# Two halves of side work in one step: transposes of a block, levels of a linear head, and a softmax head behind the last one

## The chip, the cores and the metric

The kernel runs on one core of a Trainium2 chip, in fp32 (the large products in a split form of two fp32r parts). The metric is the device time of one execution in microseconds (us), the median over executions; less is better. Names of engines: PE is TensorE, ACT is ScalarE, DVE is VectorE, POOL is GpSimd, SP is SyncE.

## The reference

Two blocks follow each other on 256 tokens of width 2048. The first has two layers, each a projection, three mixers (chunked band attention with 8 heads, gated linear attention with 4, memory attention with 4), an output projection and a layer norm. The second has a linear mixer (hgrn2, 8 heads), a softmax mixer (fox, 8 heads), a gated merge, and a feed-forward part (FFN).

```python
x = first_block(x, mem, w_in, ...)            # 2 layers
h = rms_norm(x, norm_mix_pre)
a_q, a_f, a_i, a_g, b_q, b_k, b_v, b_f, g_a, g_b = split(h @ w_in_2)
y_a = hgrn2_mixer(a_q, a_f, a_i, a_g, lb, norm_w) @ w_up_a
y_b = fox_mixer(b_q, b_k, b_v, b_f + b_fox_f) @ w_up_b
merged = sigmoid(g_a) * y_a + sigmoid(g_b) * y_b
x = x + rms_norm(merged @ w_o, norm_mix_post)
gate, up = split(rms_norm(x, norm_ffn_pre) @ w_ffn_in)
x = x + rms_norm((silu(gate) * up) @ w_ffn_down, norm_ffn_post)
# hgrn2_mixer: f = lb + (1-lb)*sigmoid(z), k = 1-f, S_t = diag(f_t) S_{t-1} + k_t^T i_t, o_t = S_t^T q_t
```

## The kernel before

All large products are one list of jobs, and `run` walks it in units. A unit is some 2.7 us of PE work: 12 rows of matmuls (lines L330 to L332) or 16 rows (L339, L340). Weights come by SP's queue; ACT rounds them to fp32r (L272) and DVE takes the rest (L273), some units ahead of their use.

Everything else is side work, written as Python generators. Each `yield d` gives up the turn and asks for the next one after `d` on a clock that `run` adds up from matmul columns (about ns of PE). After every unit `pump` lets at most two generators that are due take one step, so a step's matmuls stand between two units in PE's queue, and its other instructions go to the ends of the queues of ACT, DVE and POOL at that point. No scheduler moves them later: each engine works its queue in the order in which it was written. Side work writes to a pool of four PSUM banks that rotate (`B.bank()`): the fifth bank asked for is the first again, and its writer waits until that one has been read.

The side work around which the change turns:

- `hgrn_head` (8 heads of the second block, each in two halves t of 128 tokens). For each t: `decay_levels` puts ten POOL operations (L674 to L684) and two on ACT (absolute value L685, exponential L686) to make a tile E of eight levels; `H1` later 14 POOL products (L766, L767, "the set" below) and one more (L770 or L772); `H2` later eight PE products with E, four to a bank, each bank then masked on DVE (L782); then a DVE sum (L785), a product with the values, and `normed`: a square on ACT (L692), a power on POOL (L447), a scaling on DVE (L694), and, `R3` later, a transpose on PE (L377).
- `post_f` takes the forget gate's projection from PSUM: copy on ACT (L472), two DVE operations (L473, L484), two sigmoids on ACT (L1238, L1239), three POOL operations (L1243, L1244, L1245, "the trio" below). It is called twice per group of four heads, directly behind its product.
- `banded` and `memory_head`, softmax heads in three steps: scores and softmax, a transpose of the weights, the product with the values. Two generators of two heads each form a group.
- `merged` and `hidden`: a block of 512 columns of 256 rows is transposed in two halves of four transposes (`to_features`).

Of the kernel before, what the change touches and what calls it, by code (L numbers as in the profile page):

```python
# [52 lines left out]
R2 = 3500  # L53
# [327 lines left out]
def network(ctx, tc, a):  # L381
# [12 lines left out]
    def lv(i):  # L394
        return s(i).rearrange("p (l t) -> p l t", l=8)
# [31 lines left out]
    def main_split(src, k0, k1, cols=slice(0, S), scale=None):  # L427
        B.split_to(B.act[:, k0:k1, 0, cols], B.act[:, k0:k1, 1, cols], src, scale)
# [174 lines left out]
    def banded(q, k, v, bias, out):  # L603

        yield from B.acquire("att")
        st = B.bank()
        parts = (slice(0, 128), slice(128, 384))
        for t, cs in enumerate(parts):
            qs, ks = slice(t * P, t * P + P), slice(0, t * P + P)
            T.matmul(st[:, cs], q[:, qs], k[:, ks], start=True, stop=True)  # L610
        pt = B.ttile([P, 512], "P", N_ATT)
        nm, sm, rc = (B.stile([P, 2], x) for x in ("nm", "sm", "rc"))
        for i, cs in enumerate(parts):
            V.tensor_tensor_reduce(pt[:, cs], st[:, cs], bias(i, pt[:, cs]), -1.0, 3e38, ALU.add, ALU.min, nm[:, i:i + 1])
        for i, cs in enumerate(parts):
            A.activation(pt[:, cs], pt[:, cs], AF.Exp, bias=nm[:, i:i + 1], scale=-1.0, accum_out=sm[:, i:i + 1])
        V.reciprocal(rc, sm)
        for i, cs in enumerate(parts):
            V.tensor_scalar(pt[:, cs], pt[:, cs], rc[:, i:i + 1], None, ALU.mult)
        yield A1  # L620
        tb = B.bank()
        for j in range(3):
            T.transpose(tb[:, j * P:(j + 1) * P], pt[:, j * P:(j + 1) * P], ident)
        A.copy(pt[:, :384], tb[:, :384])
        yield A2
        ob = B.bank()
        T.matmul(ob[:, 0:128], v(0), pt[:, 0:128], start=True, stop=True)
        T.matmul(ob[:, 128:256], v(0), pt[:, 128:256], start=True, stop=False)
        T.matmul(ob[:, 128:256], v(1), pt[:, 256:384], start=False, stop=True)
        out(ob[:, :S])  # L630
        B.tokens["att"] += 1
        yield

    def memory_head(q, mk, mv, out):
        yield from B.acquire("att")
        st = B.bank()
        for t in range(2):
            T.matmul(st[:, t * S:(t + 1) * S], q[:, t * P:t * P + P], mk, start=True, stop=True)
        pt = B.ttile([P, 512], "P", N_ATT)
        nm, sm, rc = (B.stile([P, 2], x) for x in ("nm", "sm", "rc"))  # L640
        V.tensor_reduce(nm, st.rearrange("p (t m) -> p t m", t=2), AX.X, ALU.max, negate=True)
        for t in range(2):
            cs = slice(t * S, (t + 1) * S)
            A.activation(pt[:, cs], st[:, cs], AF.Exp, bias=nm[:, t:t + 1], accum_out=sm[:, t:t + 1])
        V.reciprocal(rc, sm)
        for t in range(2):
            cs = slice(t * S, (t + 1) * S)
            V.tensor_scalar(pt[:, cs], pt[:, cs], rc[:, t:t + 1], None, ALU.mult)
        yield A1
        tb = B.bank()  # L650
        for m in range(2):
            for t in range(2):
                T.transpose(tb[:, m * S + t * P:m * S + t * P + P], pt[:, t * S + m * P:t * S + m * P + P], ident)
        A.copy(pt, tb)
        yield A2
        ob = B.bank()
        for m in range(2):
            T.matmul(ob[:, :S], mv(m), pt[:, m * S:(m + 1) * S], start=m == 0, stop=m == 1)
        out(ob[:, :S])
        B.tokens["att"] += 1  # L660
        yield

# [2 lines left out]
    def decay_levels(E, b, t, scale):  # L667

        bt = b[:, t * P:(t + 1) * P]
        for l in range(6):  # L670
            st = 1 << l
            view = lambda x: x.rearrange("p (n u) -> p n u", u=2 * st)
            ref = view(bt)[:, :, st - 1:st].to_broadcast([P, P // (2 * st), 2 * st])
            G.tensor_tensor(view(E[:, l, :]), view(bt), ref, ALU.subtract)  # L674
        end = lambda c: b[:, c * 64 + 63:c * 64 + 64]
        lo, hi = slice(0, 64), slice(64, 128)
        G.tensor_scalar(E[:, 6, lo], bt[:, lo], end(2 * t), None, ALU.subtract)
        G.tensor_copy(E[:, 6, hi], bt[:, hi])
        if t == 0:
            G.tensor_scalar(E[:, 7, lo], bt[:, lo], end(0), end(1), ALU.subtract, ALU.subtract)  # L680
            G.tensor_scalar(E[:, 7, hi], bt[:, hi], end(1), None, ALU.subtract)
        else:
            G.tensor_copy(E[:, 7, lo], bt[:, lo])
            G.tensor_scalar(E[:, 7, hi], bt[:, hi], end(2), None, ALU.add)  # L684
        A.activation(E, E, AF.Abs)  # L685
        A.activation(E, E, AF.Exp, scale=-scale)  # L686
# [65 lines left out]
    def hgrn_head(q, k, b, v, mask, gain, out):  # L752

        yield from B.acquire("lin")
        for t in range(2):
            while len(B.free) < 3:
                yield 2000
            (ei,) = B.alloc(1)
            E = lv(ei)
            ts = slice(t * P, (t + 1) * P)  # L760
            decay_levels(E, b, t, 1.0)
            yield H1
            for l in range(7):
                view = lambda x: x.rearrange("p (n h u) -> p n h u", h=2, u=1 << l)
                e = view(E[:, l, :])
                G.tensor_tensor(e[:, :, 0, :], e[:, :, 0, :], view(k[:, ts])[:, :, 0, :], ALU.mult)  # L766
                G.tensor_tensor(e[:, :, 1, :], e[:, :, 1, :], view(q[:, ts])[:, :, 1, :], ALU.mult)  # L767
            if t == 0:
                kx = B.ttile([P, P], "kx", N_LIN)
                G.tensor_tensor(kx, E[:, 7, :], k[:, ts], ALU.mult)  # L770
            else:
                G.tensor_tensor(E[:, 7, :], E[:, 7, :], q[:, ts], ALU.mult)  # L772
            yield H2
            (mi,) = B.alloc(1)
            ms = lv(mi)
            for half in range(2):
                bank = B.bank().rearrange("p (l t) -> p l t", l=4)
                ls = slice(4 * half, 4 * half + 4)
                for l in range(4 * half, 4 * half + 4):
                    kk, qq = (E[:, l, :], E[:, l, :]) if l < 7 else (k[:, ts], q[:, ts])  # L780
                    T.matmul(bank[:, l % 4, :], kk, qq, start=True, stop=True)
                V.tensor_tensor(ms[:, ls, :], bank, mask[:, ls, :], ALU.mult)  # L782
                yield R2
            sc = B.ttile([P, 2, P], "sc", N_LIN)
            V.tensor_reduce(sc[:, 0, :], ms.rearrange("p l t -> p t l"), AX.X, ALU.add)  # L785
            if t == 1:
                cross = B.ttile([P, 2, P], "cross", N_LIN)[:, 0, :]
                xb = B.bank()
                T.matmul(xb[:, :P], kx, E[:, 7, :], start=True, stop=True)
                A.copy(cross, xb[:, :P])  # L790
            B.release([ei, mi])
            yield R1
            ob = B.bank().rearrange("p (e v) -> p e v", v=P)
            T.matmul(ob[:, 0, :], sc[:, 0, :], v(t), start=True, stop=t == 0)
            if t == 1:
                T.matmul(ob[:, 0, :], cross, v(0), start=False, stop=True)
            yield from normed(ob, sc, 1, gain, out(t))
        B.tokens["lin"] += 1
# [586 lines left out]
    def to_features(gi, n):  # L1385

        bank = B.bank()
        for j in range(2):
            for t in range(2):
                T.transpose(bank[:, (2 * j + t) * P:(2 * j + t + 1) * P],  # L1390
                            vt(gi)[:, t, (2 * n + j) * P:(2 * n + j + 1) * P], ident)
        return bank.rearrange("p (k t) -> p k t", t=S)
# [3 lines left out]
    def merged(c):  # L1396
        yield FH
        for n in range(2):
            main_split(to_features(st[f"gb{c}"], n), 4 * c + 2 * n, 4 * c + 2 * n + 2, scale=0.5)
            yield 1500  # L1400
        B.release([st[f"gb{c}"]])

    def merged_get(kt):
# [140 lines left out]
    def hidden(c, gi):  # L1544

        yield FH
        if len(f["h"]) <= 2 * c:
            f["h"] += B.alloc(2, F32R)
        for n in range(2):
            slot_split(f["h"][2 * c + n:2 * c + n + 1], to_features(gi, n))  # L1550
            yield 1500
        B.release([gi])

    def hidden_get(kt):
# [92 lines left out]
```

## Time and profile before

| | |
|---|---|
| time, median of 3 runs | 2407.39 us (2406.78 to 2407.83) |
| the profiled execution's own time | 2407.96 us |
| its span, first to last instruction | 2406.2 us |
| PE busy | 2390.2 us (99%) |
| PE weight loads busy | 2015.7 us (84%) |
| DVE busy | 1476.3 us (61%) |
| ACT busy | 1099.0 us (46%) |
| POOL busy | 400.8 us (17%) |
| DMA | 464.64 MB, mean 193 GB/s |
| granted PE clock | 0.999 of full |

Busy time is the sum of an engine's instructions. PE's queue holds the jobs and the side work together, so each of its gaps lengthens the execution; gaps of the other engines need not. "PE row" and a number below count the main matmuls from the start of the program (10768 in all), which places a side step in both orders.

### The profile page before, as it was taken

How to read it: one execution, taken by the hardware profiler on the slowest of the kernel's cores; microseconds unless marked ns; L12 is line 12 of the kernel's file. 1: busy time of each engine (PE TensorE's matmuls, PEld its weight loads, DVE VectorE, ACT ScalarE, POOL GpSimd, SP SyncE). 2: the span in 40 equal slices, each digit the busy share in tenths (PEclk: the TensorE clock that was granted, in tenths of full speed). 3: DMA queues.
4: the chain of work that ended last, by engine and by line, in shares of the span. 5: the costliest groups of instructions: out<-in, count | busy, mean ns of one | idle time of the engine just before them, and what ended most of it. 6: DMA issues, size and time to landing. Idle time of an engine off the chain costs nothing. (4 is left out here: it accounts for less than half of the span.)

```text
span 2406.2 us, 31460 instructions
## 1 busy us (share of the span) xinstructions
PE 2390.2 (99%) x12105; PEld 2015.7 (84%) x12105; DVE 1476.3 (61%) x1671; ACT 1099.0 (46%) x1472; POOL 400.8 (17%) x601
## 2 busy tenths in 40 slices
PE   9999999999999999999999999999999999999998
PEld 8888888888888888888888888888888888888886
DVE  6587567666855667766765656657545544554455
ACT  6444445345454553655544544445434423443433
POOL 0330010004400110364764340001000000000000
PEclk9999999999999999999999999999999999999999
DMA  9646567674656674854654666675755655555653
GB/s 327 184 149 184 173 187 262 209 239 133 188 160 186 206 252 156 275 164 125 185 161 146 201 185 194 202 242 186 242 176 180 194 185 193 201 183 177 209 192 131
DMA packets 313911, 464.64 MB, mean 193 GB/s; under 512 B 21961, under 2 KB 161569, under 8 KB 313761
## 3 DMA queue, kind: packets, MB, share of 16 engines
q1 hardware_dynamic: 312528, 459.48, 60.7%
q8 instruction: 95, 1.56, 0.3%
q0 software_dynamic: 640, 2.10, 0.2%
q10 hardware_dynamic: 592, 1.06, 0.1%
q14 instruction: 56, 0.45, 0.1%
HBM read 454.18 MB, written 8.40 MB: 192 GB/s over the span
## 5 line engine op out<-in xcount | busy, mean ns | idle before, releaser
L273 DVE TENSOR_TENSOR slot<-slot,slot 128x1024 fp32r<-128x1024 f32 x810 | 1006.9, 1287 | 190.5 <-ACT slot L272 186.7
L272 ACT CAST slot<-slot 128x1024 fp32r<-128x1024 f32 x810 | 807.8, 1046 | 266.2 <-DVE slot L273 123.6
L339 PE MATMUL main_j<-act,slot 128*128 128x512 f32 x1824 | 651.0, 400 | 0.0
L330 PE MATMUL main_j<-slot,act 128*128 128x512 f32 x1608 | 636.2, 396 | 0.0
L331 PE MATMUL main_j<-slot,act 128*128 128x512 f32 x1608 | 626.4, 390 | 2.8 <-DVE slot L273 2.8
L332 PE MATMUL main_j<-slot,act 128*128 128x512 f32 x1608 | 626.8, 390 | 0.0
L340 PE MATMUL main_j<-act,slot 128*128 128x256 f32 x1824 | 509.9, 280 | 0.0
L339 PEld LDWEIGHTS main_j<-act,slot 128*128 128x128 f32 x1824 | 342.4, 188 | 80.2 <-issue 1.1
L331 PEld LDWEIGHTS main_j<-slot,act 128*128 128x128 f32 x1608 | 302.4, 188 | 63.6 <-DVE slot L273 3.8
L332 PEld LDWEIGHTS main_j<-slot,act 128*128 128x128 f32 x1608 | 301.8, 188 | 63.9
L330 PEld LDWEIGHTS main_j<-slot,act 128*128 128x128 f32 x1608 | 302.2, 188 | 61.3 <-ACT slot L272 0.5
L340 PEld LDWEIGHTS main_j<-act,slot 128*128 128x128 f32 x1824 | 344.1, 189 | 0.8
L330 PE MATMUL main_j<-slot,slot 128*128 128x512 f32 x600 | 236.1, 394 | 0.0
L332 PE MATMUL main_j<-slot,slot 128*128 128x512 f32 x600 | 233.8, 390 | 0.0
L331 PE MATMUL main_j<-slot,slot 128*128 128x512 f32 x600 | 233.6, 389 | 0.0
L447 POOL TENSOR_TENSOR rsl<-rsl,nhalf 128x1 f32<-128x1 f32 x8 | 6.2, 775 | 991.7 <-DVE rsl L446 991.7
L332 PEld LDWEIGHTS main_j<-slot,slot 128*128 128x128 f32 x600 | 112.6, 188 | 23.8
L330 PEld LDWEIGHTS main_j<-slot,slot 128*128 128x128 f32 x600 | 112.7, 188 | 23.0
L331 PEld LDWEIGHTS main_j<-slot,slot 128*128 128x128 f32 x600 | 112.8, 188 | 22.5
L674 POOL TENSOR_TENSOR slot<-slot 128x128 f32<-128x128 f32 x144 | 79.2, 581 | 191.9 <-PE main_j L339 92.8
L354 ACT CAST slot<-bank 128x512 fp32r<-128x512 f32 (+1 forms) x30 | 15.9, 529 | 177.7 <-PE bank L377 170.7
L813 POOL TENSOR_TENSOR slot<-slot,tz 128x512 f32<-128x512 f32 x20 | 25.8, 1290 | 397.8 <-DVE tz L812 397.8
(193 smaller groups left out, 1738.4 us busy)
## 6 DMA issues: line engine op xcount, KB each, us to landing
slot<-in_w_in_dram SPq DMA_DIRECT2D x384, 512.0 KB, 4.0
slot<-in_w_ffn_in_dram SPq DMA_DIRECT2D x176, 512.0 KB, 4.6
slot<-in_w_ffn_down_dram SPq DMA_DIRECT2D x88, 512.0 KB, 4.6
slot<-in_w_out_dram SPq DMA_DIRECT2D x64, 512.0 KB, 4.7
slot<-in_w_o_dram SPq DMA_DIRECT2D x32, 512.0 KB, 4.5
slot<-in_w_mem_kv_dram SPq DMA_DIRECT2D x31, 512.0 KB, 5.9
slot<-in_w_up_b_dram SPq DMA_DIRECT2D x16, 512.0 KB, 4.6
slot<-in_w_up_a_dram SPq DMA_DIRECT2D x16, 512.0 KB, 4.4
```

Of the source, the lines that this page charges most:

```text
L272: nc.scalar.copy(h, src)
L273: nc.vector.tensor_tensor(l, src, h.bitcast(F32), ALU.subtract)
L330: nc.tensor.matmul(o, xh[:, rows], h[:, k, :], start=st, stop=False)
L331: nc.tensor.matmul(o, xh[:, rows], l[:, k, :], start=False, stop=False)
L332: nc.tensor.matmul(o, xl[:, rows], h[:, k, :], start=False, stop=en)
L339: nc.tensor.matmul(job.ps[:, f, :], h[:, k, fs], xs, start=st, stop=False)
L340: nc.tensor.matmul(job.ps[:, f, :S], l[:, k, fs], xh, start=False, stop=en)
L354: nc.scalar.copy(h, src)
L447: G.tensor_tensor(out, out, nhalf[:, :n], ALU.pow)
L674: G.tensor_tensor(view(E[:, l, :]), view(bt), ref, ALU.subtract)
L813: G.tensor_tensor(y, y, tz, ALU.mult)
```

## The change

Five `yield`s go or move, and nothing else. The two halves of a transposed block (`merged`, `hidden`) are written in one step, with a bank each. The two halves of the levels in `hgrn_head` are written in one step, and the delay `R2` (3500) follows once instead of twice. The last `yield` of `banded` and `memory_head` goes, so a generator's second head writes its scores in the same step as the first head's last product.

```diff
@@ banded, memory_head
         out(ob[:, :S])
         B.tokens["att"] += 1
-        yield
@@ hgrn_head
                 V.tensor_tensor(ms[:, ls, :], bank, mask[:, ls, :], ALU.mult)
-                yield R2
+            yield R2
             sc = B.ttile([P, 2, P], "sc", N_LIN)
@@ merged
             main_split(to_features(st[f"gb{c}"], n), 4 * c + 2 * n, 4 * c + 2 * n + 2, scale=0.5)
-            yield 1500
@@ hidden
             slot_split(f["h"][2 * c + n:2 * c + n + 1], to_features(gi, n))
-            yield 1500
```

Line numbers of `hgrn_head` and what follows are two lower in the changed kernel (L766 is L764 there, L1243 is L1241). Number and kind of the instructions on each engine stay as they were; their order changes from PE row 968 on, and the number of stretches of side work in PE's queue falls from 211 to 176.

Three places in the second block carry the steps below. The first is PE's queue at a levels step. Before, the four levels of E tile 1634 stand at PE row 5344 and the other four at row 5392, with three main units between them:

```order
L340 MATMUL main_j76_10083<-act_72,slot_1655_9887 128x256
L373 MATMUL bank_1690_10101<-slot_1634_9769 128x128 x4
L339 MATMUL main_j76_10083<-act_72,slot_1665_9935 128x512
...
L340 MATMUL main_j76_10083<-act_72,slot_1676_10010 128x256
L373 MATMUL bank_1707_10208<-slot_1634_9769 128x128 x3
L373 MATMUL bank_1707_10208<-slot_1494_8875,slot_1466_8676 128x128
L339 MATMUL main_j77_10220<-act_72,slot_1679_10036 128x512
```

After the change all eight of the same head's tile, now numbered 1680, stand at row 5392, in two banks:

```order
L340 MATMUL main_j76_10136<-act_72,slot_1689_10064 128x256
L373 MATMUL bank_1718_10267<-slot_1680_10010 128x128 x4
L373 MATMUL bank_1719_10273<-slot_1680_10010 128x128 x3
L373 MATMUL bank_1719_10273<-slot_1494_8875,slot_1466_8676 128x128
L339 MATMUL main_j77_10285<-act_72,slot_1692_10091 128x512
```

The second place is POOL's queue at the two calls of `post_f` of the second group (PE rows 5264 and 5328). Before, a decay group of ten operations stands ahead of the first trio, and between the two trios there are one power and one set:

```order
L674 TENSOR_TENSOR slot_1634_9769<-slot_1467_8677 128x128 x6
L677 TENSOR_SCALAR slot_1634_9769<-slot_1467_8677 128x64
...
L1243 TENSOR_TENSOR slot_1657_9908<-slot_1657_9908,om_1464_8672 128x512
L1244 TENSOR_TENSOR slot_1657_9908<-slot_1657_9908,lb_1463_8671 128x512
L1245 TENSOR_TENSOR slot_1658_9909<-slot_1658_9909,om_1464_8672 128x512
L447 TENSOR_TENSOR rs_1670_9961<-rs_1670_9961,nhalf_117 128x1
L766 TENSOR_TENSOR slot_1634_9769<-slot_1634_9769,slot_1466_8676 128x64
```

After it, a power and a decay group (tile 1680) stand between the trios, and the set of 1680 stands behind the second trio, followed by the next head's decay group (1709) and then a power:

```order
L1243 TENSOR_TENSOR slot_1671_9963<-slot_1671_9963,om_1464_8672 128x512
L447 TENSOR_TENSOR rs_1675_9977<-rs_1675_9977,nhalf_117 128x1
L672 TENSOR_TENSOR slot_1680_10010<-slot_1467_8677 128x128 x6
...
L1243 TENSOR_TENSOR slot_1671_9963<-slot_1671_9963,om_1464_8672 128x512
L764 TENSOR_TENSOR slot_1680_10010<-slot_1680_10010,slot_1466_8676 128x64
...
L770 TENSOR_TENSOR slot_1680_10010<-slot_1680_10010,slot_1494_8875 128x128
L672 TENSOR_TENSOR slot_1709_10218<-slot_1467_8677 128x128 x6
...
L447 TENSOR_TENSOR rs_1712_10235<-rs_1712_10235,nhalf_117 128x1
```

The third place is ACT's queue between the two calls of `post_f`. Before, no absolute value or exponential of a decay group stands between the first call's sigmoids and the second call's copy (L472); there are weight casts, a softmax head's exponentials and a square:

```order
L1239 ACTIVATE slot_1658_9909<-slot_1659_9910 128x512
L616 ACT_TABLE_LOAD
L616 ACTIVATE P_1661_9922,sm_1663_9924<-P_1661_9922,nm_1662_9923 128x128
L616 ACTIVATE P_1661_9922,sm_1663_9924<-P_1661_9922,nm_1662_9923 128x256
L272 CAST slot_1665_9935<-slot_1637_9786 128x1024
L692 ACTIVATE sc_1638_9805,ss_1669_9960<-bank_1668_9958 128x128
```

After it, the absolute value and the exponential of tile 1680 (L683, L684) stand there, ahead of three weight casts, two copies out of banks and the copy for the second call; the square of the next half (L690) stands behind the pair of tile 1709 in the same way further down the queue:

```order
L272 CAST slot_1677_9987<-slot_1650_9831 128x1024
L683 ACTIVATE slot_1680_10010<-slot_1680_10010 128x1024
L684 ACT_TABLE_LOAD
L684 ACTIVATE slot_1680_10010<-slot_1680_10010 128x1024
L272 CAST slot_1681_10023<-slot_1656_9860 128x1024
L624 COPY P_1659_9887<-bank_1687_10058 128x384
L272 CAST slot_1688_10063<-slot_1665_9919 128x1024
L354 CAST slot_1587_9522<-bank_1691_10085 128x256
L272 CAST slot_1692_10091<-slot_1669_9944 128x1024
L472 COPY slot_1672_9964<-main_j75_9993 128x512
...
L684 ACTIVATE slot_1709_10218<-slot_1709_10218 128x1024
L690 ACTIVATE sc_1696_10124,ss_1711_10234<-bank_1710_10231 128x128
```

## Rows read from the trace of the kernel before

**Rows 1.** Windows: us, then busy us and count of each engine, clock, DMA

```profile
100.00:960.00 860.00, 860.00 (x4748) 736.68 (x4747) 575.48 (x679) 402.43 (x590) 132.34 (x139) 1.00 0.62 191
1700.00:2390.00 690.00, 690.00 (x3087) 571.27 (x3086) 352.51 (x340) 272.57 (x302) 0.55 (x1) 1.00 0.59 189
```

**Rows 2.** Waits of PE by releaser: total us, times, longest

```profile
PE bank L377 <- DVE sc L694: 1.7, 1, 1.7
...
PE bank L373 <- POOL slot L767: 0.7, 1, 0.7
```

**Rows 3.** Timeline of PE in the FFN: start, us, instruction

```profile
1716.72 0.39 PE L332 MATMUL main_j<-slot,act 128*128 128x512 f32 x1
1716.96 0.60 PE L377 MATMUL bank<-ident,slot 128*128 128x128 f32 x4
...
1717.62 0.40 PE L331 MATMUL main_j<-slot,act 128*128 128x512 f32 x1
```

**Rows 4.** Timeline of PE in the second block

```profile
1125.24 0.38 PE L373 MATMUL bank<-slot,sc 128*128 128x128 f32 x2
...
1128.28 0.83 PE L373 MATMUL bank<-slot 128*128 128x128 f32 x6
1128.95 0.39 PE L373 MATMUL bank<-slot,slot 128*128 128x128 f32 x2
```

**Rows 5.** Timeline of ACT in the second block

```profile
1127.30 0.58 ACT L472 COPY slot<-main_j 128x512 f32<-128x512 f32 x1
...
1131.50 1.28 ACT L616 ACT_TABLE_LOAD   x1
1132.79 0.40 ACT L616 ACTIVATE P<-P,nm 128x128 f32<-128x128 f32 x1
...
1134.63 0.26 ACT L692 ACTIVATE sc<-bank 128x128 f32<-128x128 f32 x1
...
1136.76 0.47 ACT L624 COPY P<-bank 128x384 f32<-128x384 f32 x1
1137.13 1.05 ACT L272 CAST slot<-slot 128x1024 fp32r<-128x1024 f32 x1
1138.09 0.58 ACT L472 COPY slot<-main_j 128x512 f32<-128x512 f32 x1
```

**Rows 6.** Timeline of DVE in the second block

```profile
1127.16 0.68 DVE L782 TENSOR_TENSOR slot<-bank,slot 128x512 f32<-128x512 f32 x1
1127.76 1.21 DVE L273 TENSOR_TENSOR slot<-slot,slot 128x1024 fp32r<-128x1024 f32 x1
...
1136.72 0.29 DVE L694 TENSOR_TENSOR sc<-bank,rs 128x128 f32<-128x128 f32 x1 [0.68 <-POOL rs L447]
```

**Rows 7.** Timeline of POOL in the second block

```profile
1031.44 4.26 POOL L674 TENSOR_TENSOR slot<-slot 128x128 f32<-128x128 f32 x6 [19.03 <-DVE slot L1260]
...
1040.90 0.36 POOL L766 TENSOR_TENSOR slot<-slot,slot 128x64 f32<-128x64 f32 x1 [3.61 <-ACT slot L686]
...
1046.92 0.45 POOL L770 TENSOR_TENSOR kx<-slot,slot 128x128 f32<-128x128 f32 x1
...
1096.49 2.22 POOL L674 TENSOR_TENSOR slot<-slot 128x128 f32<-128x128 f32 x6
...
1102.24 0.36 POOL L766 TENSOR_TENSOR slot<-slot,slot 128x64 f32<-128x64 f32 x1 [2.33 <-ACT slot L686]
...
1111.19 0.46 POOL L772 TENSOR_TENSOR slot<-slot,slot 128x128 f32<-128x128 f32 x1
...
1133.37 1.04 POOL L1245 TENSOR_TENSOR slot<-slot,om 128x512 f32<-128x512 f32 x1
1136.12 0.57 POOL L447 TENSOR_TENSOR rs<-rs,nhalf 128x1 f32<-128x1 f32 x1 [1.71 <-DVE rs L446]
...
1144.19 0.46 POOL L772 TENSOR_TENSOR slot<-slot,slot 128x128 f32<-128x128 f32 x1
...
1147.60 2.02 POOL L1245 TENSOR_TENSOR slot<-slot,om 128x512 f32<-128x512 f32 x1
```

More of the change, by code (lines that the diff above doesn't have):

```diff
@@ L660, in memory_head @@
         B.tokens["att"] += 1
-        yield
     def decay_levels(E, b, t, scale):
```

## Prediction, made before the changed kernel ran

> **What bounds the kernel now.** I read the windows first. From 100 to 960 us and from 1700 to 2390 us PE is busy for all of the 860 and 690 us, at the full one of its two clock levels, 2.4 GHz [rows 1]. Nothing can be won in those stretches except by shortening PE's own list; every wait that an edit adds to PE's queue there, or in the second block between them, is added to the time. Then I read who PE waits for. In the second block's mixers it waits twice: 1.7 us for the scaling L694 and 0.7 us for a product of a set, L767 [rows 2]. These 2.4 us are all that the change could remove there. PE runs a fixed list, so the question is whether side work that stands earlier in that list is still ready in time.
>
> **What costs next to nothing.** The change adds and removes no instruction. It takes 35 stretches of side work out of PE's queue (211 to 176, counted in the orders). What does a stretch cost beside its matmuls? In the FFN 0.90 us pass from one main matmul (1716.72) over four transposes and the next one to the second behind them (1717.62), and a main step is 0.24, up to 1716.96 [rows 3]: 0.42 us are left for four transposes and all else. A fp32 side matmul of 128 columns takes 0.22 us (three, recorded as six, in 0.67, from 1128.28 to 1128.95 [rows 4]); a transpose is recorded once where such a matmul is recorded twice, so 0.11, and four fill the 0.42. I take 0.02 for a stretch, 0.7 us for 35, and allow from nothing to 0.05, 1.8 us.
>
> `merged` and `hidden` (15 steps) now put eight transposes in a row, which use two of the four side banks. Their input has to be ready at the same point as before, since the first half already needed both row halves. What hides the second half's copies on ACT and DVE is the lead of the weights: in the new order a cast L272 stands 48 to 64 PE rows ahead of the first matmul that reads it, some 10 us. If that cover were gone, each step would cost one more bank copy, about 0.47 us by the nearest row (L624, [rows 5]), 7 us in all; PE's 690 us without a gap speak against it [rows 1].
>
> The softmax heads' scores come one unit earlier. They read only q and k, long there, and in the first block PE has no gap now. The jobs that drain those heads come several units after the last step in both orders. I take zero, with up to 3 us where the scores of two heads and a levels step follow each other at PE rows 5916 to 5940 and share four banks.
>
> **Where it costs: the levels of the linear heads.** Eight levels in one step want the whole set of POOL products at the point where so far only half was wanted, and two banks at once. Since `R2` is paid once, each half of a head also ends one or two units earlier, and the next head's decay group moves up in POOL's and ACT's queues. The place where this meets something is around the two trios of the second group. I count from T, the moment when PE ends the job at PE row 5264.
>
> PE's own way. Sixteen rows take 2.82 us: from the matmul at 1125.24 (0.22) to the next side step at 1128.28 is 3.04 [rows 4]. With 0.22 for a side matmul, from row 5264 to 5328 stand 64 rows (11.3) and the side work of rows 5264, 5296 and 5312 (0.75 + 2.05 + 0.65; a transpose 0.11): PE comes to its step at row 5328 at T + 14.8.
>
> Wait A, row 5328. The step's transpose takes the bank that the first four levels of row 5296 filled, four banks ago; DVE must have masked them (L782). In DVE's order a weight operation L273 stands ahead of that, and waits for a cast that in ACT's order stands behind the absolute value and exponential of tile 1680. These wait for 1680's decay group, which on POOL stands behind the first trio and a power. From the copy L472 to the end of the trio the trace shows 7.1 us (1127.30 [rows 5] to 1134.41 [rows 7]); the power 0.57; from a decay group's first operation to the first product that reads the exponential 5.75 (1096.49 to 1102.24 [rows 7]), without a table load, which is another 1.28 [rows 5]: 7.0. Then a cast 1.05 [rows 5], L273 1.21 and L782 0.68 [rows 6]. 7.1 + 0.57 + 7.0 + 1.05 + 1.21 + 0.68 = 17.6. Wait A: 17.6 - 14.8 = 2.8 us. Bounds: 0.5 (no table load, and no L273 inside the trio's way, 1.0), and 7.2, if the trio takes the 11.5 us of the second call before (1138.09 [rows 5] to 1149.62 [rows 7]).
>
> Wait B, row 5392. After the exponential (T + 14.7) ACT has three casts and two bank copies of at most 0.47 ahead of the second call's L472: T + 18.8. The second trio ends 7.1 later, at T + 25.9, and only then POOL starts the set of 1680: 7.5 us (the power ends at 1136.69, L772 starts at 1144.19 [rows 7]), T + 33.4. PE wants the seventh level at T + 14.8 + 2.8 + 0.3 (row 5328's step) + 11.3 + 1.1 (two steps) + 1.3 (six levels) = T + 31.6. Wait B: 1.8 us. Bounds: 0.3 (a set of 6.0 us, 1040.90 to 1046.92 [rows 7]) and 7.7 (a set of 9.0, 1102.24 to 1111.19, behind a trio of 11.5).
>
> Wait C, row 5424. The transpose there needs L694 of the half whose square stands on ACT behind the exponential of tile 1709, and 1709's decay group stands on POOL behind the set of 1680 and its last product (0.46). A decay group of a first half, to the first product after the exponential, takes 9.5 us (1031.44 to 1040.90 [rows 7]); from the square to the end of L694 2.4 (1134.63 [rows 5] to 1137.01 [rows 6]). From the set's end that is 12.4 us. PE has 6.3 us of work on that way: two levels, 32 rows, one matmul. Wait C: 6.1 us. Lower bound 2.7 (the group as short as 7.0, the chain without queueing some 1.5: 0.26, 0.57, 0.29 and two small steps); the upper one is 6.1, as 9.5 is the longest of such rows here.
>
> What is queued behind these waits is PE's main list, so they add up: 10.7 us. Two other sets stand only 36 PE rows (some 8 us) behind the square whose power goes ahead of them on POOL, at rows 5140 and 6264; with the side work there and the first six levels PE is away for 10 to 11 us, and the way from the square over the power (2.1) and a set (7.5) is 9.6: zero, with up to 2 us each. The rest keep 60 rows and more.
>
> A rule speaks against this kind of edit. The Trainium skill (Perfetto Trace Analysis, "Optimizing Tensor Performance") says that independent groups of matmuls should rotate through different PSUM banks, so that emptying one overlaps the next group. By it a step that takes two of four side banks at once halves the room for that, which is wait A's mechanism; worked out, it gives A's 2.8 us and no more. Another of its rules would make the waits longer. On ScalarE: Activation LUTs ("What ACT_TABLE_LOAD costs") it gives 1.28 us for a load and 1.38 for a drain with it. The trace shows a load at 1131.50 and the next activation at 1132.79 [rows 5], no drain; with it, A and C would each grow by 1.4 and the sum by 2.8.
>
> **Sum.** 2407.96 (the profiled execution) + 10.7 - 2.4 - 0.7 = 2415.6 us. That execution stood 0.57 above the median, so I forecast 2415.0.
>
> **Rivals.**
> Not slower: POOL's groups are short. If a set takes 6.0 us, not 7.5, and a decay group with its exponential 7.0, not 9.5, then A, B and C stand at their lower bounds, 3.5 us: 2407.4 + 3.5 - 2.4 - 0.7 = 2407.8, or, with 0.05 for a stretch, 2406.7. It decides at the group of 1709: C is paid in full from 9.5 us on and is under 3 at 7.0. For it: of the sets in the rows one is as short. Against it: the square and the casts behind those groups have still to come, whatever POOL does. Chance 0.28.
> Worse: the same pattern shows a second time, around rows 5916 to 5976, where scores of two heads, a levels step and its cross product ask for eight banks in three units, and each is emptied by DVE in turn; another 3 us there, and waits A and B towards their upper bounds: 2407.4 + 7 + 7 + 6 + 3 - 3 = 2427, half way there 2421. Chance 0.15.
> The forecast itself, 2411 to 2419: 0.57.
>
> **How the numbers follow.** About 0.2% (4.8 us) is what a measurement of this kernel tells from no change. Slower by more: the forecast but for its lower end, and the worse case, 0.65. Within: the rival with the short groups and the forecast's lower end, 0.30. Faster would need more than the 3.1 us that there are to win (2.4 + 0.7), 4.2 with the larger cost of a stretch: 0.05. The range goes from 2406.5, just under that rival, to 2423, which leaves out the far end of the worse case; the likeliest case alone has 2411 to 2419.
>
> **What would show it.** In the profile after: PE without gaps from 100 to 960 and from 1700 to 2390 us, as now; three waits between some 1135 and 1175 us, a transpose for DVE's L780 or the cast ahead of it, a level for POOL's L765, a transpose for L692, together 8 to 14 us; no wait at 1137 for the old L694. On POOL the decay group of tile 1680 should end ahead of the second trio, and ACT should sit idle before its absolute value. If PE waits there for less than 3 us, the chain by ACT is wrong; if the time grows elsewhere, above all in the FFN, the cover by the weights' lead is.

## The result, and the profile after

The changed kernel takes 2424.6 us (2423.5 to 2425.3), the kernel before 2407.1: 1.0072 times the time (1.0054 to 1.0089), 17.5 us more. I had forecast 2415.0 and at most 2423. The profiled execution took 2425.3 us, its span is 2423.5, against 2407.96 and 2406.2 before.

By stretches (columns as in [rows 1]) the page after answers to [rows 1] in the first and last line; between them stand the second block's mixers and two short stretches of them:

```profile
100.00:960.00 860.00, 860.00 (x4737) 735.78 (x4736) 571.00 (x676) 400.92 (x587) 134.02 (x141) 1.00 0.61 189
960.00:1715.00 755.00, 739.82 (x3775) 625.22 (x3774) 478.73 (x581) 368.43 (x512) 240.70 (x448) 0.99 0.60 189
1143.00:1153.00 10.00, 4.88 (x20) 3.95 (x19) 6.19 (x8) 8.03 (x10) 0.00 (x0) 0.66 0.33 96
1170.00:1186.00 16.00, 9.85 (x48) 8.18 (x47) 11.78 (x16) 8.87 (x15) 8.05 (x17) 0.89 0.52 164
1700.00:2390.00 690.00, 690.00 (x3090) 572.45 (x3089) 347.42 (x338) 278.38 (x313) 0.70 (x1) 1.00 0.61 195
```

The same middle stretch of the kernel before:

```profile
960.00:1715.00 755.00, 750.89 (x3834) 633.90 (x3833) 491.36 (x589) 375.23 (x518) 260.69 (x448) 1.00 0.62 194
```

From 100 to 960 and from 1700 to 2390 us PE has no gap, as forecast. Yet in the first of these stretches it did 4737 matmuls, against 4748 before [rows 1], with 860 us of busy time in both. Between 960 and 1715 us it is busy for 11.1 us less than before, and it ran at a lower granted clock: 0.66 and 0.89 in the two short stretches, where before it was full (1.00) from 100 to 2390 us.

What PE waits for in the mixers (columns as in [rows 2], 1045 to 1300 us):

```profile
PE bank L373 <- DVE sc L783: 5.9, 3, 3.6
PE bank L377 <- ACT P L624: 4.0, 1, 4.0
PE bank L377 <- DVE sc L692: 2.6, 1, 2.6
PE bank L373 <- DVE slot L780: 1.1, 1, 1.1
PE bank L373 <- DVE rs L446: 0.6, 1, 0.6
```

The two waits of [rows 2] are gone. In their place stand 14.2 us. The timeline of PE shows where (as in [rows 4]; in brackets the idle time ahead and its releaser):

```profile
1142.88 0.28 PE L340 MATMUL main_j<-act,slot 128*128 128x256 f32 x1
1147.18 0.47 PE L377 MATMUL bank<-ident,sc 128*128 128x128 f32 x1 [4.02 <-ACT P L624]
1148.75 0.77 PE L373 MATMUL bank<-slot,kx 128*128 128x128 f32 x2 [1.10 <-DVE slot L780]
1149.17 0.77 PE L339 MATMUL main_j<-act,slot 128*128 128x512 f32 x1
...
1162.81 1.74 PE L373 MATMUL bank<-slot 128*128 128x128 f32 x14
...
1173.20 0.30 PE L377 MATMUL bank<-ident,sc 128*128 128x128 f32 x1 [2.57 <-DVE sc L692]
1179.90 0.77 PE L373 MATMUL bank<-slot,sc 128*128 128x128 f32 x2 [3.58 <-DVE sc L783]
```

These are rows 5328 (wait A), 5392 (where I had wait B: none), 5424 (wait C) and 5440, of which the prediction says nothing. ACT, as in [rows 5]:

```profile
1130.44 0.58 ACT L472 COPY slot<-main_j 128x512 f32<-128x512 f32 x1
...
1142.39 1.06 ACT L683 ACTIVATE slot<-slot 128x1024 f32<-128x1024 f32 x1 [6.06 <-POOL slot L682]
1143.46 1.28 ACT L684 ACT_TABLE_LOAD   x1
1144.76 1.06 ACT L684 ACTIVATE slot<-slot 128x1024 f32<-128x1024 f32 x1
1145.72 1.03 ACT L272 CAST slot<-slot 128x1024 fp32r<-128x1024 f32 x1
1146.65 0.47 ACT L624 COPY P<-bank 128x384 f32<-128x384 f32 x1
...
1168.21 1.06 ACT L683 ACTIVATE slot<-slot 128x1024 f32<-128x1024 f32 x1 [9.91 <-POOL slot L679]
...
1171.54 0.26 ACT L690 ACTIVATE sc<-bank 128x128 f32<-128x128 f32 x1
```

Twice ACT stands idle ahead of an absolute value, 6.06 and 9.91 us, until POOL has ended a decay group. POOL, as in [rows 7]:

```profile
1136.43 1.04 POOL L1243 TENSOR_TENSOR slot<-slot,om 128x512 f32<-128x512 f32 x1
1137.43 0.55 POOL L447 TENSOR_TENSOR rs<-rs,nhalf 128x1 f32<-128x1 f32 x1
1137.94 3.20 POOL L672 TENSOR_TENSOR slot<-slot 128x128 f32<-128x128 f32 x6
...
1153.88 1.04 POOL L1241 TENSOR_TENSOR slot<-slot,om 128x512 f32<-128x512 f32 x1 [11.53 <-ACT slot L1236]
...
1157.99 1.33 POOL L764 TENSOR_TENSOR slot<-slot,slot 128x64 f32<-128x64 f32 x1
...
1163.97 0.45 POOL L770 TENSOR_TENSOR slot<-slot,slot 128x128 f32<-128x128 f32 x1
1164.39 2.20 POOL L672 TENSOR_TENSOR slot<-slot 128x128 f32<-128x128 f32 x6
```

It is the order that the prediction describes: trio, power, decay group of tile 1680; second trio, set, decay group of 1709. And DVE, as in [rows 6], from ACT's second idle time on:

```profile
1172.77 0.29 DVE L692 TENSOR_TENSOR sc<-bank,rs 128x128 f32<-128x128 f32 x1 [0.69 <-POOL rs L447]
1172.97 1.22 DVE L273 TENSOR_TENSOR slot<-slot,slot 128x1024 fp32r<-128x1024 f32 x1
1174.11 0.68 DVE L473 TENSOR_TENSOR slot<-slot,main_j 128x512 f32<-128x512 f32 x1
1174.82 0.76 DVE L484 TENSOR_TENSOR slot<-slot,rbc 128x512 f32<-128x512 f32 x1
1175.50 1.28 DVE L780 TENSOR_TENSOR slot<-bank,slot 128x512 f32<-128x512 f32 x2
1176.70 1.26 DVE L273 TENSOR_TENSOR slot<-slot,slot 128x1024 fp32r<-128x1024 f32 x1
1177.88 1.88 DVE L783 TENSOR_REDUCE sc<-slot 128x128 f32<-128x1024 f32 x1
```

L692 ends wait C. But behind it DVE has 6.7 us of work that came late too, without a gap, and at its end the sum L783, which PE wants 2.8 us (16 rows) after C.

### The profile page after: what moved, and what is told of

Same layout as the page of the kernel before. It is cut to its first block, busy times and chain, and to the rows that moved or that the text cites. A ratio compares the mean times of both kernels' runs of the same rounds, so it can differ in the third digit from the quotient of the medians.

```text
span 2423.5 us, 31438 instructions
## 1 busy us (share of the span) xinstructions
PE 2395.9 (99%) x12105; PEld 2020.4 (83%) x12105; DVE 1466.3 (61%) x1671; ACT 1096.8 (45%) x1472; POOL 380.8 (16%) x601
## 5 line engine op out<-in xcount | busy, mean ns | idle before, releaser
L273 DVE TENSOR_TENSOR slot<-slot,slot 128x1024 fp32r<-128x1024 f32 x810 | 999.8, 1283 | 219.3 <-ACT slot L272 213.1
L332 PEld LDWEIGHTS main_j<-slot,act 128*128 128x128 f32 x1608 | 302.3, 188 | 63.3
L354 ACT CAST slot<-bank 128x512 fp32r<-128x512 f32 (+1 forms) x30 | 14.8, 532 | 158.1 <-PE bank L377 152.3
```

Source lines behind the costliest of these rows:

```text
L273: nc.vector.tensor_tensor(l, src, h.bitcast(F32), ALU.subtract)
L332: nc.tensor.matmul(o, xl[:, rows], h[:, k, :], start=False, stop=en)
L354: nc.scalar.copy(h, src)
```

## The experiments

**The parts of the change.** The queue theory is the prediction's: ACT stands idle behind POOL, and all that is behind it is late. The first rival puts the loss on two banks in one step, the second on the softmax heads. `a1_levels_only`:

```diff
                 V.tensor_tensor(ms[:, ls, :], bank, mask[:, ls, :], ALU.mult)
-                yield R2
+            yield R2
```

> Only the levels of hgrn_head in one step, the rest as before. Queue theory (ACT stands idle before the absolute value of a decay group that stands on POOL behind a trio, and the bank copies, squares and casts behind it come late): the next half's decay group stands between the two trios here too, but PE comes to the levels at row 5312, 16 rows later than in the changed kernel, and to the next levels at row 5424, 32 later, so a part of the waits remains: 2410 to 2419 us. Rival one (two banks in one step are what costs, at every levels step alike): nearly all of the loss, 2420 to 2425. Rival two (the scores that follow a softmax head directly cost): 2406 to 2408.

Measured 2417.98 us, before 2407.20 (ratio 1.0042, 1.0025 to 1.0059). `a2_levels_back` is the changed kernel with that edit undone.

> The changed kernel with the levels in two steps again. Queue theory: the set of a half stands between the trios as before and no decay group does, so ACT does not stand idle there: 2405 to 2409 us, PE's waits in the second block's mixers under 3 us. Rival one (banks): the same. Rival two (softmax heads): most of the loss stays, 2417 to 2425.

Measured 2418.45 us (1.0046, 1.0031 to 1.0061). `a3_heads_only`:

```diff
         out(ob[:, :S])
         B.tokens["att"] += 1
-        yield
```

> Only the last yield of the two softmax heads goes, the rest as before. Queue theory and rival one: 2406 to 2409 us. Rival two (softmax heads): 2417 to 2425.

Measured 2418.55 us (1.0046, 1.0031 to 1.0061). `a4_blocks_only` is the part of `merged` and `hidden`.

> Only the two halves of a transposed block in one step in merged and hidden. All theories: 15 stretches less at 0.02 to 0.07 us each, 0.3 to 1.0 us less than before, 2406.0 to 2407.2. If the weights' lead did not cover the second bank it would be up to 7 us more.

Measured 2406.80 us (0.9999, 0.9990 to 1.0009).

No one theory holds in all four. `a1` lies in the range of the queue theory alone; `a2` and `a3` lie in that of the second rival, where the queue theory had next to no loss. The blocks cost nothing that can be told from zero, as forecast. The softmax heads, for which I took zero, cost 11.3 us by themselves, the levels 10.8, and the whole change 17.5: less than their sum.

Part of the heads' loss is not a wait at all. The first block in `a3_heads_only` (columns as in [rows 1]):

```profile
100.00:960.00 860.00, 860.00 (x4739) 735.35 (x4738) 570.79 (x676) 400.79 (x587) 133.08 (x140) 1.00 0.61 190
```

PE is busy all the time at the full clock, and does nine matmuls fewer than before [rows 1]; `a1` and `a4` do 4750 and 4747. From main matmul 960 to main matmul 4000 the trace of `a3` takes 2.3 us longer than that of before; so do the changed kernel and every other run here with the heads' edit, and the runs without it take 0.0 us longer. It is a slower pace of the main matmuls, for instance 0.7 us over the 200 from 1600 on. So it comes with the heads' two `yield`s; why is not shown.

The rest is in the second block. In `a3_heads_only` the levels at row 5248 wait there, and the timelines of PE, DVE and ACT tell why:

```profile
1123.72 1.13 PE L373 MATMUL bank<-slot 128*128 128x128 f32 x8 [3.11 <-DVE slot L355]
```
```profile
1120.24 1.23 DVE L273 TENSOR_TENSOR slot<-slot,slot 128x1024 fp32r<-128x1024 f32 x1 [6.07 <-ACT slot L272]
1121.38 1.86 DVE L783 TENSOR_REDUCE sc<-slot 128x128 f32<-128x1024 f32 x1
1123.16 0.41 DVE L355 TENSOR_TENSOR slot<-bank,slot 128x256 fp32r<-128x256 f32 x1
```
```profile
1117.12 1.06 ACT L683 ACTIVATE slot<-slot 128x1024 f32<-128x1024 f32 x1 [7.45 <-POOL slot L682]
```

The scores that moved up ask for a bank of their own, so the levels' bank is now one that a head's last product filled. DVE empties it (L355) behind a sum, a weight and a cast, and the cast stands on ACT behind an absolute value that waits 7.45 us for POOL. That idle time was there before the change, 42.6 us of it between 1030 and 1300 us; no bank that PE wanted hung on it.

**The decay group on DVE.** The ten operations of `decay_levels` in `hgrn_head` go from POOL to DVE, in the changed kernel (`d1_decay_on_dve`), with the heads' part alone (`d2_heads_decay_on_dve`), in the kernel before (`d3_before_decay_on_dve`) and with the levels' part alone (`d4_levels_decay_on_dve`):

```diff
-    def decay_levels(E, b, t, scale):
+    def decay_levels(E, b, t, scale, G=G):
...
-            decay_levels(E, b, t, 1.0)
+            decay_levels(E, b, t, 1.0, V)
```

> The changed kernel, with the ten operations of a decay group in hgrn_head on DVE in place of POOL; the order of PE's list stays. Queue theory, as it stands after the first four runs (a bank is emptied late because ACT and, behind its casts, DVE stand idle until POOL has finished a decay group): ACT's waits of 5 to 10 us ahead of the absolute value go, and with them most of PE's: 2405 to 2412 us. Bank theory (more banks are asked for in one stretch than four can serve, whatever POOL does): 2418 to 2426.

> Only the two yields of the softmax heads gone (2418.55 us by itself), and the decay group on DVE. Queue theory: 2404 to 2410 us, no wait of PE for L355 at row 5248. Bank theory: 2415 to 2420.

> The kernel before, with the decay group on DVE. Queue theory: its 2.4 us of waits in the mixers of the second block shrink, 2404.5 to 2407.5. Bank theory: 2406.5 to 2408. If DVE becomes too slow with 48 us more of work, 2409 or more.

> Only the levels in one step (2417.98 us by itself), and the decay group on DVE. Queue theory: 2405 to 2411 us. Bank theory: 2415 to 2420.

Measured 2426.8, 2416.6, 2409.3 and 2419.0 us (ratios 1.0081, 1.0040, 1.0011 and 1.0050), before 2406.9. The queue theory as I had put it there falls: all four lie above its ranges, and next to nothing came back (2.0 us in `d2`). The bank theory's ranges hold `d2` and `d4` and miss `d1` by 0.8 us, so these four runs do not speak against it. ACT's waits in `d1_decay_on_dve` from 1030 to 1300 us say why it is no test of idle ACT:

```profile
ACT slot L683 <- DVE slot L682: 34.9, 6, 8.6
ACT slot L683 <- DVE slot L679: 28.4, 7, 5.4
```

ACT is idle ahead of the absolute value for 63.3 us, more than the 53.6 of the changed kernel (45.4 of them for POOL, 8.2 for a bank of PE): the group now stands in DVE's queue, behind weights and scalings that wait for others.

**How near the steps stand.** `e1_one_step_later` is the levels' part alone with `yield H2 + R2` ahead of the step; `e2_two_steps_sooner` and `f2_two_steps_farther` are the kernel before with its two steps:

```diff
                 V.tensor_tensor(ms[:, ls, :], bank, mask[:, ls, :], ALU.mult)
-                yield R2
+                yield 1750
```

(that is `e2`; in `f2` it is 5250).

> Both halves of the levels in one step, as in the run of the levels alone (2417.98 us), but one delay R2 later, at the point where the second half stood before, so that what follows a head keeps its place. Nearness theory (the loss comes because the steps of a head and the next head's stand nearer to each other): most of the loss goes, 2406 to 2411 us. Two-bank theory (it comes because one step takes two of the four side banks): 2415 to 2420.

> The kernel before with its two steps of four levels, one bank each, but with 1750 in place of R2 behind each, so that what follows a head comes about as early as with the levels in one step. Nearness theory: most of the loss of the run of the levels alone, 2412 to 2419 us. Two-bank theory: 2405 to 2409.

> The kernel before with its two steps of four levels, and 5250 in place of R2 (3500) behind each: nothing is merged, the steps of a head stand farther apart, and everything behind them moves later. Nearness theory: there is more room, 2405 to 2408 us. Place theory (what counts is where the decay groups, sets and sums fall against the two calls of post_f and against each other in the queues of POOL, ACT and DVE, and any edit that moves them by a unit or two loses the place that they had): 2411 to 2418.

Measured 2416.6 us (1.0039, 1.0024 to 1.0054), 2416.5 (1.0038, 1.0023 to 1.0053) and 2414.7 (1.0029, 1.0018 to 1.0040). Of the two theories for `e1` and `e2`, each fits one run and misses the other: with one bank a step (`e2`) or two (`e1`), it costs 9 us. So taking two banks in one step is not needed for the loss, and neither is nearness, since `f2` loses 7.5 us with the steps farther apart; there the place theory holds. In `e1` PE waits at one place (row 5376) for 7.9 and 1.1 us, and it is wait A's chain once more (timelines of PE and of ACT):

```profile
1156.35 0.47 PE L377 MATMUL bank<-ident,sc 128*128 128x128 f32 x1 [7.92 <-ACT P L624]
```
```profile
1151.56 1.06 ACT L685 ACTIVATE slot<-slot 128x1024 f32<-128x1024 f32 x1 [6.11 <-POOL slot L684]
```

In `f2` it goes through DVE: a power on POOL stands behind a trio and a whole set, PE waits 6.3 us, and DVE's timeline has

```profile
1141.55 0.29 DVE L694 TENSOR_TENSOR sc<-bank,rs 128x128 f32<-128x128 f32 x1 [5.80 <-POOL rs L447]
```

In the kernel before the power stands between trio and set at that place [rows 7].

**Taking the chain apart.** `b3_trio_on_dve` is the changed kernel with the three operations of `post_f` on DVE (`V.` for `G.`). `c1_exp_later` gives ACT the absolute value and the exponential later than POOL the group; `f1_exp_later_heads` does it in the first group's heads but the first, `f5_all_but_first` in all heads but the first; `f3_both_repairs` and `f5_all_but_first` have the trio on DVE too. With `decay_levels` left to its POOL operations in `hgrn_head`, the code of those heads reads (cut out of the whole edit):

```diff
             decay_levels(E, b, t, 1.0)
-            yield H1
+            yield 8000
+            A.activation(E, E, AF.Abs)
+            A.activation(E, E, AF.Exp, scale=-1.0)
+            yield H1 - 8000
```

> The changed kernel with the trio of post_f on DVE in place of POOL; PE's order stays. Queue theory for POOL: the decay group, the powers and the set no longer stand behind a trio of 3 to 4 us, the waits at rows 5328, 5424 and 5440 fall from 12.1 us together to under 6: 2416 to 2420 us. Nearness and bank theories: 2422 to 2427.

> The changed kernel, but ACT is given the absolute value and the exponential of a decay group of hgrn_head 8000 later than POOL its ten operations (and the set 2000 behind that, the same 10000 in all), so that ACT no longer stands idle behind POOL's decay groups; other steps move by a unit with it. Queue theory for ACT: ACT's waits for L679 and L682 of 6 to 10 us go, the casts and copies behind them and then DVE are in time: 2408 to 2414 us. Nearness and bank theories: 2418 to 2426.

> The changed kernel, with the absolute value and the exponential given to ACT 8000 later as in the run c1, but only in the second to fourth head of the first group, so that the first head's set at row 4960 is not late. Queue theory for ACT: the waits for L624, L780, L692 and L783 between rows 5300 and 5620 (14.5 us in the changed kernel) stay away as they did in c1, and the 3.9 us that c1 lost at row 4960 do not come: 2411 to 2415 us. If c1's gain was only another order of PE's steps: 2416 to 2424.

> As f1, and the trio of post_f on DVE as well. If the trio and ACT's order are two parts of one chain, the second repair adds little: within 2 us of f1. If they are two causes, 3 to 6 us less than f1.

> As f3, with the later exponential in all heads but the very first (the second group's too), since what f3 still loses stands at rows 5940 and 5976, in the second group's first head (3.6 us with the clock). Queue theory: that goes as well, 2406.0 to 2408.5 us, no more than the kernel before. If a gap of this kind only moves on to the next place: 2410 to 2413.

| | us | ratio to before | PE's waits, 1045 to 1300 us | ACT idle ahead of the absolute value, 1030 to 1300 us |
|---|---|---|---|---|
| changed kernel | 2424.6 | 1.0072 (1.0054 to 1.0089) | 14.2 | 53.6 |
| `b3_trio_on_dve` | 2416.0 | 1.0038 (1.0024 to 1.0052) | 9.1 | 44.3 |
| `c1_exp_later` | 2417.7 | 1.0044 (1.0029 to 1.0059) | 5.8 | 11.6 |
| `f1_exp_later_heads` | 2412.5 | 1.0021 (1.0012 to 1.0031) | 2.7 | 31.6 |
| `f3_both_repairs` | 2411.0 | 1.0016 (1.0007 to 1.0025) | 3.0 | 31.0 |
| `f5_all_but_first` | 2405.8 | 0.9991 (0.9982 to 1.0000) | 0.5 | 14.9 |

`b3` came out at the lower edge of its range: the waits at rows 5328, 5424 and 5440 fell from 11.3 to 4.3 us. In `c1` the waits for L624, L780, L692 and L783 are gone; what is left are five for POOL's L770, since the exponential and so the set are late for levels that are soon wanted. Its time lies above the queue theory's range all the same, 0.3 us under that of the others. `f1` keeps the first head as it was, and lies in the queue theory's range. `f3` is 1.5 us under `f1`, where `b3` was 8.6 under the changed kernel: trio and ACT's order are one chain. `f5` has all of the change in it, and in the mixers one wait:

```profile
PE bank L373 <- POOL slot L771: 0.5, 1, 0.5
```
```profile
960.00:1715.00 755.00, 754.09 (x3856) 637.85 (x3855) 499.81 (x604) 376.70 (x520) 240.58 (x436) 1.00 0.63 196
```

These edits add a step to each head, so PE's order differs by a unit here and there; `b3` alone leaves PE's order as it is. `f5` is 1.8 us under the kernel before, hardly to be told from no change, and 0.2 under its range. It still has the slower pace of the first block (2.3 us) and makes up for it in the mixers. No run has the two repairs in the kernel before, so how much of the 18.8 us between `f5` and the changed kernel would have come without the change too is not shown.

**The clock.** `k1_waits_in_ffn` and `k2_longer_waits_in_ffn` put multiplications by one ahead of the transposes in `hidden`, in the kernel `a4_blocks_only`:

```diff
+        for _ in range({0: 4, 1: 7, 2: 10}.get(c, 0)):
+            V.tensor_scalar(s(gi), s(gi), 1.0, None, ALU.mult)
```

(that is `k2`; `k1` has `{2: 3, 5: 6, 8: 10}`).

> The kernel before with merged and hidden in one step (2406.80 us), and with 3, 6 and 10 multiplications by one on DVE ahead of the transposes in the third, sixth and ninth step of hidden, so that PE waits there for some 1, 4 and 8 us in a stretch that has no waits. [...]

> The kernel before with merged and hidden in one step (2406.80 us), and with 4, 7 and 10 multiplications by one on DVE ahead of the transposes in the first, second and third step of hidden in each of the FFN's three passes: waits of PE of about 1.2, 3.3 and 5.5 us (three multiplications made 0.5), in a stretch that has no waits otherwise. Clock theory: the waits of 5.5 us, and some of 3.3, are followed by a fall of the granted clock for 3.4 or 6.8 us, each of which costs 1.2 to 2.5 us beside the wait: 2438 to 2447 us. Rival: the waits cost their own length, 2435 to 2438.

The question was whether waits in a stretch that has none are followed by a lower granted clock. `k1` came out at 2408.7 us (one execution): only the step with three multiplications exists (`c` goes to 3 at most), its three waits are 0.5 us each, and it tells nothing on the clock. `k2` took 2447.3 us (one execution), 40.5 more than `a4_blocks_only`; its nine waits add up to 30.2. The windows around six of them, of 1.2, 3.4, 5.6, 3.3, 5.6 and 5.6 us (columns as in [rows 1]):

```profile
1715.00:1735.00 20.00, 18.79 (x88) 15.41 (x87) 11.46 (x13) 6.77 (x8) 0.00 (x0) 1.00 0.59 167
1762.00:1782.00 20.00, 16.61 (x71) 13.43 (x71) 12.36 (x15) 6.79 (x8) 0.00 (x0) 0.91 0.47 133
1812.00:1832.00 20.00, 14.42 (x61) 11.84 (x60) 14.18 (x17) 6.87 (x8) 0.00 (x0) 0.83 0.46 159
2041.00:2061.00 20.00, 16.70 (x79) 13.62 (x78) 12.20 (x14) 6.76 (x8) 0.00 (x0) 1.00 0.63 206
2089.00:2109.00 20.00, 14.42 (x62) 11.87 (x62) 14.35 (x17) 6.87 (x8) 0.00 (x0) 0.91 0.51 166
2366.00:2386.00 20.00, 14.42 (x56) 11.74 (x55) 11.91 (x15) 4.95 (x6) 0.00 (x0) 0.83 0.31 100
```

The clock falls behind all three waits of 5.6 us, behind one of three of 3.3 to 3.4, and behind none of 1.1 to 1.2; the three windows left out read 1.00. Main matmul by main matmul against `a4_blocks_only`, the nine places cost 39.6 us, 9.4 more than their waits: 0.2 each where the clock stays, 1.6 to 3.0 where it falls. The rival, for which a wait costs its own length alone, falls; the time itself stands just past the upper end of the clock theory's range (2447).

## Why the prediction was wrong

**The direction and wait A.** The mechanism was right: the decay group of 1680 between the trios, ACT idle ahead of its absolute value, a transpose at row 5328 that waits. PE came there 14.8 us after T (1128.2), as worked out. The chain took 20.5 us, up to the product at 1148.75, not 17.6: ACT's copy L472 stands 2.2 us behind T, behind two casts, where I had it at T; from it to the trio's end are 7.0 us (7.1 forecast); from the group's start to the end of the exponential 7.9 (7.0). I had the wrong bank, too: the transpose waits for ACT's copy L624, the product behind it for L780. 4.0 + 1.1 = 5.1 us in place of 2.8, for a chain that was longer than worked out, inside its bounds.

**Waits B and C.** B is not there: the set took 6.0 us (1157.99 to 1163.97), its lower bound, and PE itself came to that step at T + 34.6, not 30.3. C is 2.6 us, also at its lower bound of 2.7: from the set's end to the square are 7.1 us, where I took 9.5 for the group. So the three waits that the sum names came to 7.7 us, not 10.7, while all waits came to 14.2. The place that the worse rival names, rows 5916 to 5976, shows no wait.

**The step that failed** is the one behind C: I ended each chain where PE gets its bank, and did not count what else is behind the same idle time. DVE's 6.7 us behind L692 made a wait of 3.6 us at row 5440. Three smaller waits stand where I took zero: 1.6 us for L783 at row 5528 and 0.6 for L446 at row 5116, each behind an idle time of ACT ahead of an absolute value (5.75 and 5.41 us, for POOL), and 0.7 for L783 at row 5024, which I have not followed back. Together 6.5 us that the sum does not have. "I take zero" for the softmax heads failed twice: I looked whether their scores were ready, not whose bank they push on to a late engine; and in the first block, where I looked for gaps only, PE's slower pace takes 2.3 us. Alone the heads cost 11.3 us.

**The clock** is the other missing term. At the lower level a pair of main matmuls takes some 0.68 us, not 0.35 (1149.17 to 1151.87 for four pairs, 1180.75 to 1182.78 for three, the first behind side matmuls a little longer): 2.3 us behind the waits at rows 5328 and 5440, and with the side matmuls there some 3.

**The account.** 2425.3 - 2407.96 = 17.3 us between the two profiled executions. Both traces hold all 10768 main matmuls, so they can be laid side by side: main matmul 960 starts 2.1 us later in the changed kernel, number 4000 starts 4.4 us later, 4700 3.2, 7000 18.0 and the last 17.1.

- The first 2.1 us stand ahead of anything that the change moves (PE row 968), 1.7 of them in the first 100 us, at a clock of 0.98 (1.00 before); so they belong to that execution.
- The 2.3 us up to 4000 are the first block's slower pace.
- The 1.2 us that come back up to 4700 belong to the execution before for the most part: it waits 1.3 us for a weight (L273) at row 4530, the changed one 0.4.
- The 14.8 us up to 7000 are the mixers: waits 14.2 - 2.4 = 11.8 and some 3 for the clock.
- The last 0.9 come back in the stretches of the blocks. Of these `a4_blocks_only` shows 0.4 in its time, not told from zero.

**Right:** slower, by the chain over ACT; no PE gaps in the two long stretches; the two old waits gone; the blocks hidden by the weights' lead; no drain with a table load (the load at 1143.46, 1.28 us, the next activation at 1144.76). The Trainium skill (ScalarE: Activation LUTs, "What ACT_TABLE_LOAD costs") names 1.38 us more for a drain; this trace shows none. The rule of the Trainium skill on rotating banks (Perfetto Trace Analysis, "Optimizing Tensor Performance") I had read as a price of two banks in one step. Wait A is of its kind, but `f5` takes the two banks in one step and waits 0.5 us: the price is that of the late reader, not of the step.

**Shown, and open.** That idle time of ACT behind POOL makes most of these banks and sums late is shown by the timelines of the changed kernel, `a3` and `e1`; and the waits go with it in `c1`, `f1` and `f5`, which move steps on PE as well. It is not proportional: the kernel before has 42.6 us of that idle time and loses 2.4, the changed kernel has 45.4 for POOL and waits 14.2, `b3` has 44.3 and waits 9.1. So what counts must be what stands behind it when it falls; that the order before had it in a good place is argued from `e1`, `e2` and `f2`, not shown by a run of its own. In `f2` the late engine is POOL with a power, without idle time of ACT. Why the first block's pace falls with the heads' edit, and why both parts together cost less than their sum, stays open. No run had more side banks, so whether a fifth would do as much stays open.

## What to carry to other kernels

When a step moves on an in-order queue, follow the idle time on to all that is behind it on that engine and on those it feeds, up to the next few things that the bounding engine wants, and not to the first only. In this kernel, whose bounding engine is hardly ever idle, five small moves of side work by a unit or two cost 7 to 11 us each, whatever they were meant for. So keep such an order, or else first remove the waits at the head of a queue: here the activation was given to ACT 8000 later, when POOL had its input ready, and with the trio on DVE the changed kernel gained 18.8 us. And a stretch without gaps is not a stretch without loss: count the bounding engine's instructions in it too, before and after.

## Unexpected

A wait of the PE queue costs more than its length. Behind the first wait of 3.4 us in `k2` the granted clock is at the lower of the two levels, 1.2 GHz, and a main step takes 0.43 us in place of 0.23 (six steps from 1767.89 to 1770.45): 1.2 us lost in those six. The fall came behind three of three waits of 5.6 us, one of three of 3.3 to 3.4, none of three of 1.1 to 1.2; in the changed kernel behind those of 4.0 and 3.6 us, and not behind that of 2.6. I had taken the clock as full, since the kernel before shows no fall in its mixers.
